# Other matmul durations in the planner of a two-network kernel

## The chip, the core and the metric

The kernel runs on one core of a Trainium2 chip. The metric is the time of one launch on the device in microseconds (us), the median over several runs. Five engines share the work of the core: TensorE (PE) multiplies matrices and transposes, VectorE (DVE) and ScalarE (ACT) work element by element, GpSimd (POOL) does a few element-wise steps, and SyncE (SP) starts the transfers from and to memory. Each engine works its own row of instructions strictly in order; semaphores make it wait for the others.

## The reference

Two networks run one after the other on 256 tokens of width 1024, all in fp32. The first has two layers of three attentions side by side (dilated, latent and differential) and an MLP with squared ReLU. The second has four layers whose mixers are retention, conformer convolution, short convolution and retention again, each followed by such an MLP.

```python
def conformer_conv_mixer(x, w_pw1, b_pw1, w_dw, b_dw, ln_g, ln_b, w_pw2, b_pw2):
    h = x @ w_pw1 + b_pw1
    a, gate = jnp.split(h, 2, axis=-1)
    h = a * jax.nn.sigmoid(gate)
    h = causal_depthwise_conv(h, w_dw) + b_dw
    ...
    hf = (hf - mean) * lax.rsqrt(var + LN_EPS) * ln_g.astype(F32) + ln_b.astype(F32)
    h = jax.nn.silu(hf).astype(x.dtype)
    return h @ w_pw2 + b_pw2

def second_block(x, positions, norm_g, ...):
    for i in range(DEPTH_2):
        ...
        x = x + rms_norm(h, norm_g[i, 1])
        h = squared_relu_mlp(rms_norm(x, norm_g[i, 2]), mlp_w1[i], mlp_w2[i])
        x = x + rms_norm(h, norm_g[i, 3])
    return x
```

## The kernel before

The 256 tokens are two tiles of 128, called t=0 and t=1 here. The weights stream through the core in units of up to 128 x 1024 fp32. A unit arrives in a tile `raw` (4 of them), ACT copies it to `whi` (8), rounded to the faster matmul type fp32r, and DVE subtracts the two to get the rest, `wlo` (8). Lines 716 to 727, `prefetch`, do this. Activations are split in the same way into a high and a low tile `t4k` (lines 801 to 812). A product is then three matmuls: high by high, high by low, low by high. They gather in PSUM tiles `acc` (4) or `wk` (4).

The conformer (lines 1384 to 1513) makes its 1024 channels in 8 blocks of 128. A block's gated input is an `s2k` tile; the 31 taps of its convolution are shared out by the table `CONV` (line 24): ACT multiplies some taps and POOL adds them, PE does some by diagonal matrices (`dg`, `s2k`), and DVE does the others with one `SCALAR_TENSOR_TENSOR s1k<-s2k,cv,s1k` per tap. A last addition `s1k<-s1k,s1k` joins the parts. The blocks are 256 tokens wide except the last ones (third entry 1 in `CONV`), which are done 128 tokens at a time. PE then transposes the channels of one t back (`wk<-ident,s1k`), DVE takes their statistics (`BN_STATS`) and the normalized z (`TENSOR_SCALAR s2k<-wk,col,col`; the second half of z is ACT's), PE transposes z (`wk<-ident,s2k`), ACT applies silu, and the result is split into `t4k`. The product with `w_pw2` (called pw2 here, lines 786 to 799) takes 8 units, first all of t=0 and then all of t=1, and the residual x is updated from it.

No order is written out by hand. Every operation is recorded first, with a cost in ns from `cost` (line 293) that depends on engine, operation and size. `deadlines` (line 366) adds the costs of the recorded PE operations up to a time at which each PE operation is due, and goes back through the dependences to give every other operation a due time `dl`; an operation may not start earlier than 60,000 ns before its due time. `schedule` (line 389) then plays the program through: of each engine's ready operations it takes the one that can start first, and among equals the one that is due first. It hands out the buffers in that order too, and `pe_end` models PE's slower clock after pauses. `emit` (line 536) writes the instructions in that order, so the whole profile carries one line number, 546, and the groups are told apart by their tiles. The numbers behind a tile's name in the orders below are the tile's running number there, and differ between two plans.

Of the kernel before, what the change touches and what calls it, by code (L numbers as in the profile page):

```python
# [18 lines left out]
P = 128  # L19
# [265 lines left out]
class Rec:  # L285
# [7 lines left out]
    def cost(self, op, outs, ins):  # L293
        fn = op.name
        if fn == "dma_start":
            n = max(v.arr.size for v in outs + ins) * 4
            op.dma = n / 360.0
            return 60.0, 2000.0
        o = outs[0]
        n = int(np.prod(o.shape[1:]))  # L300
        n_in = max([int(np.prod(v.shape[1:])) for v in ins] + [n])
        lat = LAT[op.eng]
        psum = any(v.vt.psum for v in ins + outs)
        if op.eng == "tensor":
            if fn == "transpose":
                return 2 * o.shape[1] / 2.4 + 2.5, lat
            f32 = op.kw["lhsT"].vt.dtype == F32
            return ((4 if f32 or n < 256 else 1) * max(n, P)) / 2.4 + 2.5, lat
        if op.eng == "scalar":
            ptr = sum(isinstance(op.kw.get(k), V) for k in ("scale", "bias", "accum_out"))  # L310
            return 94 + n * 0.8333 + 93 * ptr - (43 if psum else 0), lat
        if op.eng == "gpsimd":
            if ALU.pow in (op.kw.get("op"), op.kw.get("op1")):
                return 234 + 230.0 * n, lat
            if fn == "memset":
                return 40 + n * 0.6, lat
            return 160 + n * 2.1, lat
        if fn == "reciprocal":
            return 69 + 6.25 * n, lat
        if fn == "scalar_tensor_tensor":  # L320
            return 129 + 1.042 * n, lat
        if fn == "tensor_scalar":
            ptr = sum(isinstance(a, V) for a in op.args[2:])
            return 69 + 60 * ptr + (1.042 if psum else 0.52) * n, lat
        if fn in ("tensor_copy", "memset"):
            return 69 + (1.042 if psum else 0.52) * n, lat
        return 69 + 1.042 * n_in, lat
# [1334 lines left out]
```

## Time and profile before

| | us |
|---|---|
| median of 3 runs | 1993.25 |
| lowest and highest run | 1992.52, 1994.31 |
| span of the profiled execution | 1991.4 |
| PE busy | 1949.0 (98%) |
| DVE busy | 1335.8 (67%) |
| ACT busy | 1051.1 (53%) |
| POOL busy | 159.1 (8%) |

The span runs from the first to the last instruction of the profiled execution; the runs' times also hold what lies around it, 1.85 us between the span and the median. No time of its own is listed for the profiled execution beside its span. Busy shares are an average over the whole span. Instructions of one engine overlap a little, so a row's duration is somewhat longer than the distance to the next row.

### The profile page before, as it was taken

The numbers are of one execution on the slowest core, as the hardware profiler recorded it, in microseconds if no ns is written. First come the engines' busy times: TensorE is split into PE (matmuls) and PEld (weight loads), VectorE is DVE, ScalarE is ACT, GpSimd is POOL, SyncE is SP. The second block draws the span as 40 slices with busy tenths as digits, with TensorE's granted clock in tenths as the row PEclk, the third lists the DMA queues.
The fourth block names the chain that finished last, engine by engine and source line by source line (L and its number), as shares of the span: only waits on it lengthen the run. The fifth ranks groups of instructions, "written<-read, shape, count | busy, mean of one in ns | idle before, by whom it ended". The sixth has DMA issues, their size and how long they took to land.

```text
span 1991.4 us, 30668 instructions
## 1 busy us (share of the span) xinstructions
PE 1949.0 (98%) x11696; PEld 1721.8 (86%) x11696; DVE 1335.8 (67%) x2169; ACT 1051.1 (53%) x1757; POOL 159.1 (8%) x233
## 2 busy tenths in 40 slices
PE   8999999999999999999997799999999999999998
PEld 7879998878998888899877689989899889888997
DVE  7866556886556776755589975567755577757554
ACT  7555545555545335645486655455545453555452
POOL 2200002100000000000047400000000000000000
PEclk9999999999999999999998899999999999999999
DMA  7256664246555555465631265646465655455552
GB/s 238 85 168 204 188 197 146 76 152 208 189 198 183 174 165 192 165 198 189 210 129 48 80 226 186 200 159 217 164 202 189 201 170 169 160 192 178 191 184 91
DMA packets 95763, 341.44 MB, mean 171 GB/s; under 512 B 10624, under 2 KB 10880, under 8 KB 95616
## 3 DMA queue, kind: packets, MB, share of 16 engines
q1 hardware_dynamic: 95616, 339.49, 52.6%
q8 instruction: 91, 1.49, 0.3%
q14 instruction: 56, 0.46, 0.1%
HBM read 338.40 MB, written 1.05 MB: 170 GB/s over the span
## 4 chain that ended last, share of the span: by engine, by line
PE 90%; DVE 6%; issue 1%; POOL 1%; DMA 1%; ACT 1%; SPq 0%; POOLq 0%; DVEq 0%; ACTq 0%
PE wk L546 47%; PE acc L546 43%; DVE s1k L546 4%; DVE s2k L546 1%; POOL s2k L546 1%; DMA raw<-in_w 1%; ACT s2k L546 0%; DVE wlo L546 0%; DMA x<-in_x 0%; DVE col L546 0%; DVE t4k L546 0%; DVE dg L546 0%; POOL s1k L546 0%; ACT whi L546 0%; SPq L546 0%
## 5 line engine op out<-in xcount | busy, mean ns | idle before, releaser
L546 DVE TENSOR_TENSOR wlo<-raw,whi 128x1024 fp32r<-128x1024 f32 (+3 forms) x639 | 774.0, 1217 | 538.2 <-ACT whi L546 533.6
L546 ACT CAST whi<-raw 128x1024 fp32r<-128x1024 f32 (+3 forms) x639 | 656.5, 1034 | 734.7 <-PE wk L546 374.5
L546 PE MATMUL wk<-t4k,whi 128*128 128x256 f32 x3712 | 662.8, 282 | 12.4 <-DVE s2k L546 8.8
L546 PEld LDWEIGHTS wk<-t4k,whi 128*128 128x128 f32 x3712 | 573.8, 190 | 22.0 <-DVE s2k L546 9.6
L546 PE MATMUL wk<-t4k,wlo 128*128 128x256 f32 x1856 | 510.7, 282 | 0.0
L546 PE MATMUL acc<-whi,r2k 128*128 128x512 f32 x1440 | 410.3, 394 | 0.0
L546 PE MATMUL acc<-whi,t4k 128*128 128x512 f32 (+2 forms) x1312 | 391.4, 387 | 5.9 <-ACT t4k L546 2.1
L546 PEld LDWEIGHTS wk<-t4k,wlo 128*128 128x128 f32 x1856 | 346.6, 190 | 0.1
L546 PEld LDWEIGHTS acc<-whi,r2k 128*128 128x128 f32 x1440 | 264.8, 188 | 54.6
L546 PEld LDWEIGHTS acc<-whi,t4k 128*128 128x128 f32 x1312 | 239.7, 189 | 48.5 <-ACT t4k L546 3.2
L546 PE MATMUL acc<-wlo,r2k 128*128 128x512 f32 x720 | 227.8, 393 | 0.0
L546 PE MATMUL acc<-wlo,t4k 128*128 128x512 f32 (+2 forms) x656 | 227.7, 386 | 0.0
L546 PE MATMUL wk<-whi,t4k 128*128 128x512 f32 x512 | 163.9, 398 | 0.0
L546 PEld LDWEIGHTS acc<-wlo,r2k 128*128 128x128 f32 x720 | 135.2, 188 | 31.1
L546 PEld LDWEIGHTS acc<-wlo,t4k 128*128 128x128 f32 x656 | 123.1, 190 | 20.1
L546 POOL TENSOR_TENSOR col<-col,mhalf 128x1 f32<-128x1 f32 (+1 forms) x48 | 38.3, 806 | 1157.1 <-DVE col L546 1156.8
L546 PEld LDWEIGHTS wk<-whi,t4k 128*128 128x128 f32 x512 | 95.8, 188 | 21.8 <-ACT t4k L546 0.4
L546 PE MATMUL wk<-wlo,t4k 128*128 128x512 f32 x256 | 98.7, 395 | 0.0
L546 PE MATMUL wk<-s2k,s2k 128*128 128x64 f32 (+6 forms) x492 | 85.3, 308 | 4.1 <-DVE s2k L546 3.6
L546 PEld LDWEIGHTS wk<-s2k,s2k 128*128 128x128 f32 (+2 forms) x492 | 72.6, 197 | 16.5 <-DVE s2k L546 4.0
L546 ACT ACTIVATE t4k<-wk,cv 128x128 fp32r<-128x128 f32 x256 | 72.4, 379 | 16.2 <-PE wk L546 15.9
L546 DVE SCALAR_TENSOR_TENSOR t4k<-wk,cv,t4k 128x128 fp32r<-128x128 f32 x256 | 72.4, 343 | 10.5 <-ACT t4k L546 9.6
(126 smaller groups left out, 1366.2 us busy)
## 6 DMA issues: line engine op xcount, KB each, us to landing
raw<-in_w SPq DMA_DIRECT2D x599, 512.0 KB, 4.2
raw<-in_w SPq DMA_DIRECT2D x26, 384.0 KB, 3.2
row<-in_rows SPq DMA_DIRECT2D x11, 512.0 KB, 5.0
raw<-in_w SPq DMA_DIRECT2D x8, 288.0 KB, 2.8
raw<-in_w SPq DMA_DIRECT2D x4, 432.0 KB, 4.8
kcs<-in_kc SPq DMA_DIRECT2D x2, 768.0 KB, 7.4
x<-in_x SPq DMA_DIRECT2D x4, 256.0 KB, 6.3
out_dram<-x SPq DMA_DIRECT2D x4, 256.0 KB, 2.0
```

The costliest lines, as they stand in the source:

```text
L546: op.dma = fn(*[res(a) for a in op.args], **{k: res(a) for k, a in op.kw.items()})
```

## The change

One line of the planner's `cost` becomes another. It gives the duration of a matmul with n output columns, in ns; `f32` is true for full fp32 operands and false for fp32r.

```diff
             if fn == "transpose":
                 return 2 * o.shape[1] / 2.4 + 2.5, lat
             f32 = op.kw["lhsT"].vt.dtype == F32
-            return ((4 if f32 or n < 256 else 1) * max(n, P)) / 2.4 + 2.5, lat
+            return (4 * max(n, 64) / 2.4 + 5.0 if f32 else n * 0.4434 + 4.5), lat
```

| matmul | before, ns | after, ns |
|---|---|---|
| fp32r, 512 columns | 215.8 | 231.5 |
| fp32r, 384 columns | 162.5 | 174.8 |
| fp32r, 288 columns | 122.5 | 132.2 |
| fp32r, 256 columns | 109.2 | 118.0 |
| fp32, 256 columns | 429.2 | 431.7 |
| fp32, 128 columns | 215.8 | 218.3 |
| fp32, 64 columns | 215.8 | 111.7 |

Instructions, operands and arithmetic stay as they are. What changes is the order on the engines and which buffer of a pool an operation gets. Of DVE's rows some 960 operations stand at another place, of PE's some 1990, of ACT's some 520; most moves are by a few places. Three places are shown.

The first is DVE's row in the conformer, around the gated input of the last channel blocks (`s2k<-wk,s1k 128x512`), where the subtractions that make `wlo` of the pw2 units stand. Rows of one tap that repeat are left out. Before, one such subtraction stands there:

```order
L546 TENSOR_TENSOR s1k_821<-s1k_821,s1k_829 128x256
...
L546 TENSOR_TENSOR s1k_553<-s1k_553,s1k_557 128x256
...
L546 TENSOR_TENSOR s1k_214<-s1k_214,s1k_814 128x256
L546 TENSOR_TENSOR s2k_409<-wk_110,s1k_535 128x512
L546 SCALAR_TENSOR_TENSOR s1k_804<-s2k_112,cv,s1k_804 128x256
L546 TENSOR_TENSOR wlo_608<-raw_96,whi_121 128x1024
L546 SCALAR_TENSOR_TENSOR s1k_8647<-s2k_84,cv,wk_165 128x128
```

and after the change four:

```order
L546 TENSOR_TENSOR wlo_156<-raw_96,whi_121 128x1024
L546 SCALAR_TENSOR_TENSOR s1k_833<-s2k_452,cv,s1k_833 128x256
L546 TENSOR_TENSOR wlo_338<-raw_100,whi_425 128x1024
...
L546 TENSOR_TENSOR wlo_418<-raw_86,whi_357 128x1024
L546 TENSOR_TENSOR s2k_421<-wk_133,s1k_541 128x512
...
L546 TENSOR_TENSOR wlo_348<-raw_92,whi_200 128x1024
L546 TENSOR_TENSOR s2k_452<-wk_163,s1k_541 128x512
L546 SCALAR_TENSOR_TENSOR s1k_818<-s2k_108,cv,s1k_818 128x256
L546 SCALAR_TENSOR_TENSOR s1k_541<-s2k_88,cv,wk_133 128x128
```

The three others of the four stood behind t=0's `BN_STATS` before, in the stretch where t=1's last taps run.

The second place is PE's row in the same layer, at the beginning of the pw2 product of t=0. The three `wk<-ident,s1k` are the transposes of t=1's last channel blocks. Before, 19 matmuls of pw2 stand ahead of them, the last ones here:

```order
L546 MATMUL acc_273<-whi_539,t4k_176 128x512
L546 MATMUL acc_129<-whi_539,t4k_176 128x512
L546 MATMUL acc_273<-whi_355,t4k_359 128x512
L546 MATMUL wk_480<-ident,s1k_549 128x128
L546 MATMUL wk_480<-ident,s1k_557 128x128
L546 MATMUL wk_480<-ident,s1k_547 128x128
L546 MATMUL acc_129<-whi_355,t4k_359 128x512
```

and after the change 9:

```order
L546 MATMUL acc_173<-whi_425,t4k_123 128x512
L546 MATMUL acc_173<-wlo_338,t4k_123 128x512
L546 MATMUL acc_275<-whi_425,t4k_123 128x512
L546 MATMUL wk_515<-ident,s1k_560 128x128
L546 MATMUL wk_515<-ident,s1k_8732 128x128
L546 MATMUL wk_515<-ident,s1k_828 128x128
L546 MATMUL acc_275<-wlo_338,t4k_123 128x512
```

The transposes moved from the fourth unit's first product to the second unit's.

The third place is DVE's row at the start, in the first attention layer, where the latent attention's compressed q and kv (`acc`, 384 and 128 columns) are scaled by their norms (`col`). Before:

```order
L546 TENSOR_TENSOR wlo_127<-raw_86,whi_148 128x864
L546 TENSOR_TENSOR wlo_216<-raw_92,whi_121 128x864
L546 TENSOR_SCALAR col_280<-col_137,keep_187 128x1
L546 TENSOR_TENSOR wlo_157<-raw_96,whi_265 128x576
L546 TENSOR_SCALAR col_280<-col_161,keep_192 128x1
L546 TENSOR_SCALAR col_301<-col_286,keep_187 128x1
L546 SCALAR_TENSOR_TENSOR s2k_112<-acc_129,col_137,sm_102 128x384
```

and after the change:

```order
L546 TENSOR_TENSOR wlo_260<-raw_92,whi_121 128x864
L546 TENSOR_TENSOR wlo_156<-raw_96,whi_257 128x576
L546 TENSOR_TENSOR wlo_277<-raw_100,whi_264 128x576
L546 TENSOR_SCALAR col_290<-col_137,keep_191 128x1
L546 TENSOR_SCALAR col_294<-col_281,keep_234 128x1
L546 SCALAR_TENSOR_TENSOR keep_177<-col_113,col_161 128x1
L546 TENSOR_SCALAR col_281<-col_288,keep_191 128x1
L546 TENSOR_SCALAR col_113<-col_296,keep_234 128x1
L546 SCALAR_TENSOR_TENSOR s2k_280<-acc_129,col_137,sm_102 128x384
```

Two 576-wide subtractions now stand ahead of the first `TENSOR_SCALAR`, where one stood behind it. On PE the transposes of `s2k` stand two 288-wide matmuls earlier.

## Rows read from the trace of the kernel before

**Rows 1.** The page: busy us and instructions by engine; then the chain's shares.

```profile
PE 1949.0 (98%) x11696; PEld 1721.8 (86%) x11696; DVE 1335.8 (67%) x2169; ACT 1051.1 (53%) x1757; POOL 159.1 (8%) x233
...
PE 90%; DVE 6%; issue 1%; POOL 1%; DMA 1%; ACT 1%; SPq 0%; POOLq 0%; DVEq 0%; ACTq 0%
```

**Rows 2.** By window: length, busy PE, PEld, DVE, ACT, POOL, clock, DMA, GB/s.

```profile
1050.00:1100.00 50.00, 38.51 (x241) 36.37 (x241) 49.38 (x79) 30.07 (x63) 38.50 (x49) 0.87 0.09 31
1100.00:1150.00 50.00, 39.78 (x191) 31.18 (x191) 45.68 (x93) 32.55 (x76) 17.45 (x33) 0.86 0.32 108
1150.00:1200.00 50.00, 49.94 (x311) 44.13 (x310) 33.98 (x43) 28.40 (x40) 1.46 (x1) 1.00 0.64 211
```

**Rows 3.** Waits of PE by releaser: us in total, times, longest us.

```profile
PE wk L546 <- DVE s2k L546: 14.5, 4, 4.5
PE wk L546 <- DVE s1k L546: 8.4, 5, 3.7
...
PE wk L546 <- POOL s2k L546: 1.0, 5, 0.3
```

**Rows 4.** The chain in order of time: start us, us, what, with its count.

```profile
27.18 5.59 DMA raw<-in_w
...
178.42 5.57 PE acc L546 x24
183.99 5.64 PE wk L546 x48
```

**Rows 5.** DVE's timeline at the start: start us, us, instruction, [idle before, releaser].

```profile
21.04 1.06 DVE L546 TENSOR_TENSOR wlo<-raw,whi 128x864 fp32r<-128x864 f32 x1 [0.42 <-PE acc L546]
22.36 0.21 DVE L546 TENSOR_SCALAR col<-col,keep 128x1 f32<-128x1 f32 x1 [0.26 <-ACT s2k L546]
22.49 0.75 DVE L546 TENSOR_TENSOR wlo<-raw,whi 128x576 fp32r<-128x576 f32 x1
```

**Rows 6.** PE's timeline at the start.

```profile
24.82 0.49 PE L546 MATMUL wk<-ident,s2k 128*128 128x128 f32 x3
```

**Rows 7.** DVE's timeline at the end of the conformer.

```profile
1093.55 0.35 DVE L546 SCALAR_TENSOR_TENSOR s1k<-s2k,cv,wk 128x128 f32<-128x128 f32 x1 [0.62 <-POOL s1k L546]
...
1113.80 0.80 DVE L546 TENSOR_SCALAR s2k<-wk,col,col 128x512 f32<-128x512 f32 x1
1114.52 0.34 DVE L546 SCALAR_TENSOR_TENSOR s1k<-s2k,cv,s1k 128x128 f32<-128x128 f32 x1
...
1119.83 0.68 DVE L546 TENSOR_TENSOR t4k<-s2k,t4k 128x512 fp32r<-128x512 f32 x1
...
1125.09 0.28 DVE L546 TENSOR_TENSOR s1k<-s1k,s1k 128x128 f32<-128x128 f32 x1
```

**Rows 8.** DVE's groups from 1093 to 1136 us: shapes, count, busy us, mean ns.

```profile
L546 DVE TENSOR_TENSOR wlo<-raw,whi 128x1024 fp32r<-128x1024 f32 x7 | 8.7, 1244 | 0.5 <-ACT whi L546 0.5
```

**Rows 9.** PE's timeline at the end of the conformer.

```profile
1118.22 0.80 PE L546 MATMUL acc<-whi,t4k 128*128 128x512 f32 x1 [1.18 <-ACT t4k L546]
1118.82 0.63 PE L546 MATMUL acc<-wlo,t4k 128*128 128x512 f32 x1
1119.24 0.63 PE L546 MATMUL acc<-whi,t4k 128*128 128x512 f32 x1
...
1120.56 1.65 PE L546 MATMUL acc<-whi,t4k 128*128 128x512 f32 x3 [0.26 <-DVE t4k L546]
...
1125.95 0.49 PE L546 MATMUL wk<-ident,s1k 128*128 128x128 f32 x3
...
1134.96 0.50 PE L546 MATMUL acc<-whi,t4k 128*128 128x512 f32 x1 [0.91 <-ACT t4k L546]
...
1137.18 0.72 PE L546 MATMUL acc<-whi,t4k 128*128 128x512 f32 x2 [1.01 <-DVE t4k L546]
```

**Rows 10.** DVE's groups from 1028 to 1062 us.

```profile
L546 DVE SCALAR_TENSOR_TENSOR s1k<-s2k,cv,s1k 128x256 f32<-128x256 f32 x31 | 24.4, 838 | 0.0
L546 DVE TENSOR_TENSOR wlo<-raw,whi 128x1024 fp32r<-128x1024 f32 x3 | 4.7, 1565 | 0.0
```

## The prediction

> **What bounds the kernel now.** I read the busy shares first, then the chain that ended last, then the span in pieces of 50 us, and only then single rows. TensorE (PE) is busy 1949.0 of 1991.4 us and the chain lies on it for 90% [rows 1]. A new order of the same instructions can win or lose only where PE stands still or runs at its lower clock. In most pieces there is no such place: from 1150 to 1200 us PE is busy 49.94 of 50 at a granted clock of 1.00. Two pieces stand out, 1050 to 1100 with 38.51 busy and a clock of 0.87, and 1100 to 1150 with 39.78 and 0.86 [rows 2]. That is the conformer. The reader is to see there that VectorE (DVE) is the full engine instead, 49.38 of 50. The list of PE's waits by releaser says the same: 14.5 us in 4 waits for DVE s2k tiles, 8.4 us in 5 for DVE s1k tiles, and hardly anything else but the load of x at the start; the attention's largest item, POOL s2k, is 1.0 us in 5 waits [rows 3].
>
> **Do the new numbers fit?** In the MLP 24 matmuls of 512 columns take 5.57 us, 232 ns each, and 48 of 256 columns take 5.64, 117.5 ns each [rows 4]. The old formula gives 215.8 and 109.2 ns, the new one 231.5 and 118.0. So the planner's PE becomes some 7% slower and true to the trace. The Trainium skill, page "TensorE: Matmul & The Clock Gate", section "Back-to-back issue gap", speaks against it: it gives about 131 ns for 512 columns in a sustained stream and says that N/2.4 + 2.5, the old formula, over-counts there. By that page the new numbers would be further off, not nearer; this case's trace does not agree, with its 232 ns.
>
> What follows from a truer PE is not that PE gets faster. The planner now thinks that PE has more work ahead of each point, so relative to PE everything on the other engines is due at other moments, and some of it changes place.
>
> **The change part by part.**
>
> MLPs, retention, short convolution: PE has no waits there [rows 2], the instructions are the same, so 0. The last instructions of every engine but POOL stand in the same order, so the tail is 0 as well.
>
> The start (first attention layer). Before, the scaling of the compressed q begins with the `TENSOR_SCALAR col` at 22.36, and one 576-wide wlo of 0.75 us follows it at 22.49, hidden while POOL takes the power [rows 5]. After, two such wlo stand ahead of the first `TENSOR_SCALAR`. They can begin when the 864-wide wlo of 21.04 ends at 22.10 [rows 5] and take 0.7 each, so the `TENSOR_SCALAR` would start at 23.5 instead of 22.36 if both their copies are there by then (+1.2), and at 22.8 if only the first counts (+0.5). PE's three transposes, which met no wait at 24.82 [rows 6], stand two 288-wide matmuls earlier, 2 x 0.13 by width from [rows 4]. Together a wait of 0.6 to 1.3 us. Against it: the chain goes on over a weight load of 5.59 us at 27.18 [rows 4], which begins when a wlo frees its raw tile, and the wlo now run earlier, by up to 0.7. So the start is worth -0.5 to +1.3; I take +0.6. The rest of the attention I put at 0, with 1.0 us either way, the size of its largest waits [rows 3].
>
> The conformer. Here DVE's row is the path. Up to the z of tokens 0-127 (the `TENSOR_SCALAR s2k<-wk,col,col` at 1113.80 [rows 7]) the DVE has three more 1024-wide wlo and three more 128-wide taps ahead of it than before; what was there otherwise is the same set. A wlo here takes 1.244 us [rows 8], so 3 x 1.24 = 3.7, and the three taps, 0.34 each by the row at 1114.52 [rows 7] and overlapping a little, 0.8. Taken off is the idle time of 0.62 at 1093.55, where DVE waited for POOL [rows 7]: a row that comes later meets POOL done. Sum +3.9. PE's first pw2 matmul waits for that z over ScalarE (1.18 us for ACT t4k at 1118.22 [rows 9]), so it moves from 1118.22 to about 1122.1.
>
> In the stretch from 1028 to 1062 three such wlo took 1.565 each, and the 256-wide taps 0.838 [rows 10], while POOL adds products beside them. The moved wlo land further on, between 1081 and 1092, with POOL still at work. I stay with 1.24, since a wlo that takes the slow moment leaves the taps behind it a quicker one; 1.565 is the upper bound, 3 x 0.32 = 1.0 more. The Trainium skill has this in "SBUF — State Buffer", section "Who interferes with whom": a DVE instruction with two SBUF inputs contends with a GpSimd instruction that reads SBUF. The trace agrees, with 1.565 against 1.244.
>
> Then the end of the conformer on PE. The three transposes of tokens 128-255 (`wk<-ident,s1k`, at 1125.95, no wait [rows 9]) stood behind 19 pw2 matmuls and now stand behind 9. PE works its row in order, so all that follows is queued behind them, and they need the last tap's sum. That `s1k<-s1k,s1k` at 1125.09 [rows 7] has one more wlo and one t4k (0.68 at 1119.83, same group) ahead of it: +1.24 +0.6 -0.62 = +1.2, so it ends at 1126.6. PE gets there at 1122.1 + 9 x 0.43 + 0.26 = 1126.3; 0.43 is what a 512-column matmul takes from 1118.82 to 1119.24, PE's level of 1.2 GHz after the waits before it, against 0.23 from [rows 4] at 2.4 GHz. That leaves a wait of 0.3 to 0.5; I take 0.4, and 0 to 2 for the range.
>
> What is given back: before, PE waited 0.91 for ACT t4k and 1.01 for DVE t4k of tokens 128-255 [rows 9]. Their z has the same DVE work ahead of it as before, and their t4k now stands ahead of four 512-wide additions and a column, while PE comes 4.3 us later. Both waits are then over before PE is there: -1.9. Conformer: 3.9 + 0.4 - 1.9 = +2.4, within -3 (below) and +7.
>
> Sum: 0.6 + 2.4 = +3.0 us. On the profiled execution that is 1991.4 + 3.0 = 1994.4 of span; the median of the runs, 1993.25, stands 1.85 over that span, so 1996.25, rounded 1996.2.
>
> **The rivals.** A measurement of this kernel can tell 0.2%, 4.0 us, from no change: under 1989.3 is faster, over 1997.2 slower.
>
> (a) Faster, 1988.8. The three wlo cost nothing, because DVE is held up by POOL in that stretch anyway and the tokens' z comes when it did; then the two waits of 1.92 go, the 0.62 goes, the 1.18 and 0.26 ahead of the first pw2 matmuls go [rows 9], and the start gains its 0.5: -4.5. For it: taps of 0.838 next to a busy POOL show much lost time there. Against it: DVE has hardly a gap from 1050 to 1100 (49.38 of 50), and an instruction that stands in a full row pushes all behind it.
>
> (b) Slower, 2000.5. The early transposes block PE. The three wlo take 1.565 (4.7, +0.8 of taps = 5.5), POOL's idle does not go, and the last sum comes 2.2 later, so PE waits 1.5 at the transposes and runs 8 more matmuls at 0.43 instead of 0.23 (1.6) behind that wait; 1.9 are given back, the start costs 0.6: +7.3. It decides from the point where the last sum ends after PE has done its 9 matmuls; by the sum above the two are 0.3 us apart, so it is near. The lengths of waits after which PE was at its lower level support it (1.18 us, and 0.43 per matmul behind it), the 0.91 and 1.01 with no such stretch behind them speak against it.
>
> (c) No change, 1993.25. The planner's new numbers move rows where other engines have room, and the later z is met by PE having the same total work. For it: 98% of PE. Against it: the three wlo ahead of a z that PE waits for.
>
> **How the numbers follow.** Forecast 0.44, (a) 0.19, (b) 0.20, (c) 0.17. Of the forecast a quarter lies over 1997.2. Slower by over 0.2%: 0.11 + 0.19 = 0.30. Faster: 0.14 of (a). Within 0.2%: 0.33 + 0.17 + 0.05 + 0.01 = 0.56. The range reaches from just under (a) to (b)'s value, 1988.5 to 2000.5, and leaves out half of (b) and the lower part of (a).
>
> **What would show it.** Right: PE busy as before outside the conformer; the row of the first `acc<-whi,t4k` in the conformer some 4 us later against the start of the pw1 matmuls, with three or four wlo rows ahead of the first statistics; no wait for t4k of the second tokens; a wait under 1 us at the three `wk<-ident,s1k`. (a) would show the first pw2 matmul no later than before; (b) a wait of over 1 us at those transposes and matmuls at 0.43 apart behind it. The prediction falls if PE's waits move by more than 2 us in the attention layers, or if DVE's stretch from 1028 to 1093 gets shorter or longer by more than the wlo.

## The result and the profile after

The changed kernel takes 2014.2 us in the median (2012.2 to 2021.84), against 1993.78 before in the same series: a ratio of 1.0112, with a 95% interval of 1.0100 to 1.0124. It is some 20 us slower, where 3 us were forecast. The span of its profiled execution is 2011.1 us against 1991.4.

The page of the changed kernel, to be read beside [rows 1]: PE's busy time first, then the chain by engine and by what it ran on.

```profile
PE 1957.8 (97%) x11696; PEld 1724.6 (86%) x11696; DVE 1326.0 (66%) x2169; ACT 1046.0 (52%) x1757; POOL 155.3 (8%) x233
...
PE 89%; DVE 6%; ACT 2%; POOL 1%; issue 1%; DMA 1%; SPq 0%; DVEq 0%; POOLq 0%; ACTq 0%
PE wk L546 47%; PE acc L546 43%; DVE s1k L546 3%; DVE wlo L546 1%; DVE s2k L546 1%; POOL s2k L546 1%; ACT s2k L546 1%; DVE t4k L546 1%; ACT whi L546 0%; DMA raw<-in_w 0%; POOL col L546 0%; DVE x L546 0%; DMA x<-in_x 0%; ACT s1k L546 0%; ACT t4k L546 0%
```

These shares hide the loss: every share moved by a point at most. Of the 19.7 us of span, 8.8 are in PE's busy time (1957.8 against 1949.0), since slow and short-stalled matmuls count as busy, and 10.9 in its idle time. The waits by releaser say more (compare [rows 3]):

```profile
PE wk L546 <- DVE s2k L546: 23.7, 5, 8.6
PE wk L546 <- DVE s1k L546: 6.3, 6, 3.9
...
PE wk L546 <- POOL s2k L546: 2.2, 5, 0.5
PE wk L546 <- DVE t4k L546: 2.2, 1, 2.2
PE acc L546 <- ACT whi L546: 2.0, 1, 2.0
PE wk L546 <- DVE x L546: 1.8, 4, 0.9
```

The DVE s2k item, the conformer's, went from 14.5 to 23.7, while DVE s1k fell from 8.4 to 6.3. Three items were not there before in this size: t4k with `wk`, x, and POOL s2k, which doubled. All but 0.3 us of these lie outside the conformer.

To see where the time went I summed, stage by stage, what each matmul took beyond the usual distance to the next one for its kind (the 35th percentile over all kernels of this study), from the starts of all 11,696 matmul rows. That counts waits, short stalls and slow stretches alike. A stage ends at the last transposes of x. Each row of these tables comes from the one profiled execution of a kernel, and its sum differs from the difference of the medians by up to 3.7 us ("outside it alone" below: 16.5 against 20.2), so a us or two between two rows says nothing. The loss against before, in us:

| kernel | attention 1 | attention 2 | conformer | short conv. | all other | sum |
|---|---|---|---|---|---|---|
| the changed kernel | 4.6 | 2.5 | 4.8 | 4.1 | 3.4 | 19.4 |

The other 3.4 are mostly 1.6 in the second MLP, 1.1 in the MLP ahead of the conformer and 1.0 in the one behind it. So the loss is not one stall but many, and three quarters of it lie outside the conformer, where the prediction had put 0.6.

**The short convolution** shows a joint in full. PE's timeline, with its wait in brackets:

```profile
1352.68 1.32 PE L546 MATMUL wk<-ident,x 128*128 128x128 f32 x8 [0.85 <-DVE x L546]
1353.83 0.38 PE L546 MATMUL wk<-ident,s1k 128*128 128x128 f32 x2
1356.38 0.77 PE L546 MATMUL wk<-whi,t4k 128*128 128x512 f32 x1 [2.16 <-DVE t4k L546]
1356.94 0.63 PE L546 MATMUL wk<-wlo,t4k 128*128 128x512 f32 x1
1357.37 0.63 PE L546 MATMUL wk<-whi,t4k 128*128 128x512 f32 x1
```

PE waits for x of the second 128 tokens, then for its split, 3.0 us together, and the matmuls behind follow at 0.43 instead of 0.23 us, the 1.2 GHz level: the granted clock is 0.52 from 1356 to 1359.5 us and 0.99 in the 3.5 us behind. Before, the same transposes of x met no wait:

```profile
1335.94 0.60 PE L546 MATMUL wk<-ident,x 128*128 128x128 f32 x4
1336.29 0.48 PE L546 MATMUL wk<-whi,t4k 128*128 128x512 f32 x1
1336.61 0.60 PE L546 MATMUL wk<-ident,x 128*128 128x128 f32 x4
```

Why x comes late is seen on ScalarE. First ScalarE before, then after the change; `s2k<-acc` takes the sums of squares of the MLP's result for the second tokens, from which x is updated:

```profile
1331.30 0.60 ACT L546 ACTIVATE s2k<-acc 128x512 f32<-128x512 f32 x1
...
1332.76 0.60 ACT L546 ACTIVATE s2k<-acc 128x512 f32<-128x512 f32 x1
1333.23 0.21 ACT L546 ACTIVATION_READ_ACCUMULATOR s2k<-acc 128x1 f32 x1
1333.33 2.00 ACT L546 CAST whi<-raw 128x1024 fp32r<-128x1024 f32 x2
```

```profile
1346.60 1.09 ACT L546 CAST whi<-raw 128x1024 fp32r<-128x1024 f32 x1
1347.54 0.65 ACT L546 ACTIVATE s2k<-acc 128x512 f32<-128x512 f32 x1
1348.03 0.25 ACT L546 ACTIVATION_READ_ACCUMULATOR s2k<-acc 128x1 f32 x1
1348.12 0.64 ACT L546 ACTIVATE s2k<-acc 128x512 f32<-128x512 f32 x1
```

After the change a weight copy of 1.09 us stands ahead of the first square; before, both copies stood behind the last. VectorE does the same one step later. Before, and then in the changed kernel:

```profile
1333.56 0.26 DVE L546 TENSOR_SCALAR col<-col,col,keep 128x1 f32<-128x1 f32 x1
...
1334.52 1.40 DVE L546 SCALAR_TENSOR_TENSOR x<-s2k,col,x 128x512 f32<-128x512 f32 x2
```

```profile
1348.84 1.21 DVE L546 TENSOR_TENSOR wlo<-raw,whi 128x1024 fp32r<-128x1024 f32 x1
1349.97 0.26 DVE L546 TENSOR_SCALAR col<-col,col,keep 128x1 f32<-128x1 f32 x1
...
1351.87 1.41 DVE L546 SCALAR_TENSOR_TENSOR x<-s2k,col,x 128x512 f32<-128x512 f32 x2 [0.44 <-POOL col L546]
```

After the change a weight split of 1.21 us stands ahead of the column that the update of x needs. PE is in no hurry for these weights: counted by columns in the rows up to 1346.60, ScalarE had copied 409.4 units and PE had used 403.6, so the copy was for a unit some six ahead. x is needed next.

**The conformer.** PE's timeline at its longest wait, and at the beginning of pw2 (compare [rows 9]), and VectorE's row that explains the first:

```profile
1101.15 1.22 PE L546 MATMUL wk<-s2k,dg 128*128 128x256 f32 x2 [8.59 <-DVE s2k L546]
...
1136.56 0.79 PE L546 MATMUL acc<-whi,t4k 128*128 128x512 f32 x1 [1.19 <-ACT t4k L546]
...
1140.56 0.76 PE L546 MATMUL wk<-ident,s1k 128*128 128x128 f32 x3
```

```profile
1086.38 0.81 DVE L546 SCALAR_TENSOR_TENSOR s2k<-s2k,cv 128x256 f32<-128x256 f32 x1 [4.95 <-ACT s2k L546]
...
1092.17 1.48 DVE L546 TENSOR_TENSOR wlo<-raw,whi 128x1024 fp32r<-128x1024 f32 x1
```

VectorE, which before had no gap above 0.62 us from 1028 to 1093 us [rows 7], runs dry for 4.95 us: it waits for the sigmoid of a gated input, ScalarE's `s2k<-s2k,cv 128x256`. The sigmoid's own input is VectorE's `s2k<-wk,s1k`, done at 1080.70. VectorE's row of it, then ScalarE's rows up to the sigmoid, after the change; and last the sigmoid of the same block before:

```profile
1080.03 0.67 DVE L546 TENSOR_TENSOR s2k<-wk,s1k 128x512 f32<-128x512 f32 x1
```

```profile
1081.14 1.03 ACT L546 CAST whi<-raw 128x1024 fp32r<-128x1024 f32 x1
1082.86 1.33 ACT L546 ACTIVATE s1k<-s2k,cv 128x256 f32<-128x256 f32 x3 [0.69 <-POOL s1k L546]
1084.49 0.51 ACT L546 ACTIVATE s1k<-s2k,cv 128x256 f32<-128x256 f32 x1 [0.30 <-POOL s1k L546]
1084.91 1.03 ACT L546 CAST whi<-raw 128x1024 fp32r<-128x1024 f32 x1
1085.84 0.51 ACT L546 ACTIVATE s2k<-s2k,cv 128x256 f32<-128x256 f32 x1
```

```profile
1071.78 0.51 ACT L546 ACTIVATE s2k<-s2k,cv 128x256 f32<-128x256 f32 x1 [3.33 <-DVE s2k L546]
```

Before, ScalarE stood idle for 3.33 us until the input came and took it at once. After, two weight copies of 1.03 us and four taps, which waited 1.0 us for POOL, stood ahead of the sigmoid, and it began 5.1 us after its input was done. A full engine had become an engine with a hole, and the work behind the hole (the three weight splits, the taps) came later. PE's last transposes of x ahead of the conformer, before and after, give the point to count from:

```profile
1011.92 0.60 PE L546 MATMUL wk<-ident,x 128*128 128x128 f32 x4
```

```profile
1022.72 0.60 PE L546 MATMUL wk<-ident,x 128*128 128x128 f32 x4
```

From there the first pw2 matmul starts after 113.8 us (1136.56) in place of 106.3 (1118.22 in [rows 9]), 7.5 later. Summed over VectorE's rows from the last of these transposes to the z of the first tokens, its idle time grew from 2.5 to 9.2 us, and its work by only 0.9. The three splits and three taps of the forecast do stand ahead of that z, but two of the splits were done before the stretch began, and the 75 taps of 256 columns took 48.0 us in place of 52.1.

### The profile page after: what moved, and what is told of

Read it like the earlier page. It is cut to its first block, busy times and chain, and to the rows that moved or that the text cites. A ratio compares the mean times of both kernels' runs of the same rounds, so it can differ in the third digit from the quotient of the medians.

```text
span 2011.1 us, 30644 instructions
## 1 busy us (share of the span) xinstructions
PE 1957.8 (97%) x11696; PEld 1724.6 (86%) x11696; DVE 1326.0 (66%) x2169; ACT 1046.0 (52%) x1757; POOL 155.3 (8%) x233
## 3 DMA queue, kind: packets, MB, share of 16 engines
HBM read 338.40 MB, written 1.05 MB: 169 GB/s over the span
## 4 chain that ended last, share of the span: by engine, by line
PE 89%; DVE 6%; ACT 2%; POOL 1%; issue 1%; DMA 1%; SPq 0%; DVEq 0%; POOLq 0%; ACTq 0%
PE wk L546 47%; PE acc L546 43%; DVE s1k L546 3%; DVE wlo L546 1%; DVE s2k L546 1%; POOL s2k L546 1%; ACT s2k L546 1%; DVE t4k L546 1%; ACT whi L546 0%; DMA raw<-in_w 0%; POOL col L546 0%; DVE x L546 0%; DMA x<-in_x 0%; ACT s1k L546 0%; ACT t4k L546 0%
## 5 line engine op out<-in xcount | busy, mean ns | idle before, releaser
L546 PEld LDWEIGHTS wk<-t4k,whi 128*128 128x128 f32 x3712 | 575.3, 190 | 19.5 <-DVE s2k L546 10.9
L546 PE MATMUL wk<-whi,t4k 128*128 128x512 f32 x512 | 168.3, 400 | 3.2 <-DVE t4k L546 2.2
L546 POOL TENSOR_TENSOR col<-col,mhalf 128x1 f32<-128x1 f32 (+1 forms) x48 | 33.6, 708 | 1177.0 <-DVE col L546 1171.0
L546 PEld LDWEIGHTS wk<-s2k,s2k 128*128 128x128 f32 (+2 forms) x492 | 72.4, 192 | 16.5 <-DVE col L546 3.6
```

The costliest lines, as they stand in the source:

```text
L546: op.dma = fn(*[res(a) for a in op.args], **{k: res(a) for k, a in op.kw.items()})
```

## The experiments

Every kernel differs from before or from the changed kernel in the planner alone, so all compute the same. Four theories are named in the expectations. M: the old formula's too fast PE gave the plan a margin. C: each new order is a fresh draw, whatever the change. F: the 64-column fp32 price does the harm. Y, formed after the traces of the first two groups: with a true PE the planner lets weight copies and splits go ahead of short chains.

### Which durations, and where they act

The first two kernels change the line for one kind of operand each:

```diff
-return ((4 if f32 or n < 256 else 1) * max(n, P)) / 2.4 + 2.5, lat
+return (((4 if f32 or n < 256 else 1) * max(n, P)) / 2.4 + 2.5 if f32 else n * 0.4434 + 4.5), lat
```

> Only the fp32r matmuls get the fitted duration, the fp32 ones keep the old formula. Theory M (margin): the old formula made PE some 7% too fast in the plan, which left every chain on the other engines a margin on the chip; a plan with a true PE has none. The fp32r matmuls carry nearly all of PE's planned time, so about 2010 to 2016. Theory C (chance): any change of the costs draws a new order, and the time falls anywhere from 1985 to 2020, with no tie to which costs were changed. Theory F (the 64-column fp32 matmul, 215.8 to 111.7 ns, is what harms): about 1994.

Measured: 2016.79 us, 1.0116 (1.0101 to 1.0131), 0.8 us above M's range and far from F's 1994. With fp32 alone (the two branches the other way round):

> Only the fp32 matmuls get the new formula (64 columns 215.8 to 111.7 ns, the others 2.5 ns more); fp32r keeps the old one. Theory M: PE's planned time hardly changes, so 1992 to 1997. Theory F: 2010 to 2016. Theory C: anywhere from 1985 to 2020.

Measured: 2001.81 us, 1.0042 (1.0027 to 1.0057): slower too, but 6.9 of it in the conformer and nothing in the short convolution. F falls. M missed too, by 5 us: it had it at no more than 1997.

In the next the due times are added up with the old durations and only the play-through uses the new ones:

```diff
+op.due = ((4 if f32 or n < 256 else 1) * max(n, P)) / 2.4 + 2.5
+return (4 * max(n, 64) / 2.4 + 5.0 if f32 else n * 0.4434 + 4.5), lat
...
-                t += op.cost
+                t += getattr(op, "due", op.cost)
```

> The due times are added up with the old durations, and only the play-through, which decides when PE is free and what is ready, uses the new ones. If the loss comes from the play-through (theory M), about 2010 to 2016, with PE waiting 2 us for t4k of the second tokens in the short convolution again. If it comes from the priorities that the due times set, about 1994. Theory C: anywhere from 1985 to 2020.

Measured: 2009.15 us, 1.0083 (1.0066 to 1.0100), 0.9 below M's range. PE's waits in it, one line of them:

```profile
PE wk L547 <- DVE t4k L547: 2.2, 1, 2.2
```

The wait of 2.2 us for t4k is there again, so the new play-through is enough to make it, without the new due times. The opposite pairing, new due times with the old play-through, was not run.

### How slow, and how much is chance

```diff
-return ((4 if f32 or n < 256 else 1) * max(n, P)) / 2.4 + 2.5, lat
+return ((4 if f32 or n < 256 else 1) * max(n, P)) / 2.4 + 2.5 + 0.5, lat
```

> The old formula plus 0.5 ns per matmul, 0.3% of PE's planned time: far too little to matter as a margin. Theory M and theory F: 1991 to 1997. Theory C: anywhere from 1985 to 2020, since hundreds of instructions change place here too.

Measured: 1997.36 us, 1.0020 (1.0010 to 1.0029), 0.4 above M's range. Then the whole old formula times a factor:

> The old formula times 1.07 for every matmul and transpose: PE as slow in the plan as the fitted numbers make it (planned PE time 1915.8 us against 1910.2), without the fitted numbers' proportions. Theory M (what counts is how slow PE is in the play-through): 2009 to 2017, with the losses at the same places as in the changed kernel: first attention 3 to 5 us, second 1.5 to 3, short convolution 3 to 5. Theory C (each order is a fresh draw): anywhere from 1990 to 2020, the losses at other places.

Measured: 2011.78 us, 1.0093 (1.0078 to 1.0108). The time and the attentions' losses are as M said; the short convolution lost 2.1, less than its 3 to 5.

> The old formula times 1.03. Theory M: between, 1998 to 2007, if the loss grows with the planned slowness; theory C: no order between 1.00, 1.03 and 1.07.

Measured: 2001.45 us, 1.0041 (1.0026 to 1.0056).

> The old formula times 0.97, PE still faster in the plan. Theory M: outside the conformer no loss, in all 1988 to 1997. Theory C: anywhere from 1990 to 2015.

Measured: 1999.09 us, 1.0033 (1.0021 to 1.0046): 2 us slower than M said, and with losses of 5.0 us outside the conformer, where M had none. Two more nudges, asked later for the spread:

> The old formula minus 0.5 ns per matmul. How much of the 20 us is simply that the order of before is a good draw among its neighbours? If chance is small (a few us, as with plus 0.5 ns: 3.7): 1992 to 1999. If it is as large as the change's own loss: over 2005.

Measured: 1996.0 us, 1.0014 (1.0004 to 1.0023).

> The old formula plus 1 ns per matmul (0.6% of PE's planned time). The same question: 1992 to 2000 if chance is small, over 2005 if it is as large as the loss.

Measured: 1993.93 us, 1.0001 (0.9992 to 1.0010).

So orders that differ from before in nothing that matters take 0.5 to 4 us more, and two that do not make PE slower (x 0.97, fitted fp32 only) take 6 and 8. Chance explains some us, not 20, and the 8 us of x 1.03 alone would prove nothing. From 1.00 over 1.03 to 1.07 and to the fitted numbers the loss grows (0, 8, 19, 20 us), and with 1.07 it sits where the changed kernel has it, although the proportions of the durations are the old ones. Loss against before by stage, in us, worked out as above:

| kernel | attention 1 | attention 2 | conformer | short conv. | all other | sum |
|---|---|---|---|---|---|---|
| changed | 4.6 | 2.5 | 4.8 | 4.1 | 3.4 | 19.4 |
| fitted fp32r only | 5.5 | 2.8 | 3.0 | 4.1 | 7.1 | 22.5 |
| new play-through, old due times | 3.4 | 1.9 | 1.5 | 2.8 | 6.4 | 16.0 |
| old x 1.07 | 4.1 | 2.5 | 2.8 | 2.1 | 4.2 | 15.7 |
| old x 1.03 | 4.3 | 0.6 | -0.5 | 0.5 | 3.3 | 8.2 |
| old x 0.97 | 1.0 | -0.1 | 0.1 | 0.4 | 3.7 | 5.1 |
| fitted fp32 only | 1.7 | 0.0 | 6.9 | 0.0 | 2.0 | 10.6 |
| old + 0.5 ns | 0.2 | -1.2 | 3.7 | 0.4 | 0.0 | 3.1 |
| old - 0.5 ns | 0.0 | 0.7 | 1.9 | 0.2 | 2.2 | 5.0 |
| old + 1 ns | 0.7 | -1.7 | 0.8 | 0.3 | 1.6 | 1.7 |

The reader is to see the sum less the conformer's column. In the first five rows, with a slow planned PE, it is 8.7 to 19.5 us, in the five others, as fast as before or nearly, -0.6 to 5.0. The orders of the tables below keep to this (10.3 to 16.7 and -2.5 to 1.6). Single columns are less clean: at x 1.03 attention 1 loses 4.3, the second attention and the short convolution hardly anything. The conformer's column does not follow the planned slowness: it moves by up to 6.9 us with any change, in both groups. Chance (C) is enough to explain it; outside it the planned slowness (M) tells the orders apart.

### What a true PE takes away: a margin at handoffs, or the order of weight work

Theory M in its plain form says that a handoff to PE needs some tenths of a us more in the plan.

```diff
-TO_PE = 110.0
+TO_PE = 300.0
```

> The fitted durations as in the changed kernel, but the plan's extra delay from any engine to PE (TO_PE) is 300 ns in place of 110. If the loss is a missing margin of some tenths of a us at each handoff to PE, this gives it back: 1995 to 2004. If it is that other work (the weight splits) is already taken up when a short chain becomes ready, a handoff delay changes little: 2008 to 2016.

Measured: 2009.31 us, 1.0084 (1.0068 to 1.0099). The attentions lose less than in the changed kernel (2.4 and -0.8), the short convolution still 3.8, all other stages 9.3. As a whole the remedy fails.

The rows of the short convolution above gave theory Y. The greedy step of `schedule` takes, for an engine, the operation that can start first. With a PE that is too fast in the plan the end of the MLP comes a little sooner, the squares are startable as soon as ScalarE is free, and being due earlier they go first. With a slower PE they are not startable yet at that moment, a weight copy is, and it blocks ScalarE for 1.05 us. This is read from the planner's code and the two orders; no run holds the plan's own times. PE's end need not be all of it: VectorE reads the same two `acc` tiles, the code lets no two engines at one PSUM tile at a time, and these reads (`s2k<-acc,row`) stand ahead of both squares in the changed kernel (1345.97) and behind the first square before (1331.59). On the chip the old order costs nothing: the square began at 1331.30 without a noted wait. The test lets only the weight work step back:

```diff
-                key, s = min((c[1], c[0]) for c in lst if c[0] <= s0 + SLACK.get(e, 0.0))
+                wait = 600.0 if e in ("scalar", "vector") and any(vt.tag == "raw" for vt in ops[min(lst)[1][1]].vts) else 0.0
+                key, s = min((c[1], c[0]) for c in lst if c[0] <= s0 + wait)
```

> The fitted durations, and one more rule in the plan: a weight copy on ScalarE or a weight split on VectorE steps back for up to 600 ns if an operation that is due earlier becomes startable in that time. Theory Y (yield): the old, too fast PE made short chains look startable a little sooner, so that no weight copy or split was put ahead of them; with a true PE the planner fills the gap with one (1.05 us on ScalarE, 1.2 us on VectorE) and the chain behind it comes late. Then this gives back the losses at the joints: short convolution 4 us, second MLPs and conformer head about 3 to 4, part of the attentions, in all 1996 to 2005, and no wait of PE for t4k or x at the joints. If the loss comes from something else that a true PE takes away (theory M without this mechanism), 2009 to 2018.

Measured: 2007.35 us, 1.0072 (1.0055 to 1.0089), 2.4 above Y's range and 1.7 below the other. ScalarE at the same joint, in this kernel:

```profile
1340.88 0.64 ACT L547 ACTIVATE s2k<-acc 128x512 f32<-128x512 f32 x1
...
1342.05 0.60 ACT L547 ACTIVATE s2k<-acc 128x512 f32<-128x512 f32 x1
1342.55 0.19 ACT L547 ACTIVATION_READ_ACCUMULATOR s2k<-acc 128x1 f32 x1
1342.64 1.99 ACT L547 CAST whi<-raw 128x1024 fp32r<-128x1024 f32 x2
```

The copies are behind the squares as before, the short convolution's loss is 0.6 us instead of 4.1, and PE waits there neither for x nor for t4k. The other traces agree. A weight copy stands directly ahead of both squares in the changed kernel and in fp32r only, new play-through, x 1.07, handoff 300 and "outside it alone" below, which lose 2.1 to 4.4 us in the short convolution. In the ten orders with no copy ahead of or between the squares the loss there is at most 0.6; in the two with one copy between them (yield 300, without and with handoff 300) it is 0.8 and 2.0. For the short convolution Y is shown. For the conformer it is not: VectorE's wait for a sigmoid is gone with the rule, but it is absent also in three slow orders without the rule (fp32r only, new play-through, x 1.07). The same rule with half the time:

> The same with 300 ns. Theory Y: part of the way, 1998 to 2009; otherwise 2009 to 2018.

Measured: 2004.68 us, 1.0057 (1.0042 to 1.0072), inside the range, but no less is given back than with 600 ns.

> The old formula with the 300 ns rule. Theory Y: the fast PE of the old formula already keeps the weight work behind the chains, so nothing is left to give back: 1989 to 1999, the spread of a new order in the conformer. If the rule is worth something by itself: under 1988.

Measured: 1991.68 us, 0.9991 (0.9982 to 1.0001), no difference that can be told.

> The old formula with the rule that the weight work steps back for up to 600 ns, where 300 gave 1991.68. If the rule is a gain by itself, 1985 to 1991; if 300 was a neutral redraw, 1990 to 1998.

Measured: 1995.75 us, 1.0012 (1.0003 to 1.0022). On the old formula the rule is a redraw, no gain, as Y says.

The same table for these:

| kernel | attention 1 | attention 2 | conformer | short conv. | all other | sum |
|---|---|---|---|---|---|---|
| fitted, handoff 300 | 2.4 | -0.8 | 3.9 | 3.8 | 9.3 | 18.6 |
| fitted, yield 600 | 3.0 | 1.7 | 1.2 | 0.6 | 5.0 | 11.5 |
| fitted, yield 300 | 5.4 | 2.5 | 1.8 | 0.8 | 3.1 | 13.6 |
| fitted, yield 300, handoff 300 | 4.7 | 1.6 | 2.7 | 2.0 | 2.2 | 13.2 |
| old, yield 300 | 0.3 | -0.2 | -0.8 | 0.1 | -2.7 | -3.3 |
| old, yield 600 | 2.0 | 1.2 | 0.2 | 0.1 | -2.4 | 1.1 |

The last test joins the two remedies:

> The fitted durations with both remedies: the 300 ns rule for the weight work, which gave back the short convolution, and the plan's delay to PE at 300 ns, which gave back half of the attentions (in the run with that alone, 2.4 for 4.6 us and -0.8 for 2.5). If they are two separate causes they add: 1996 to 2003. If they were luck of two orders, it stays at 2004 to 2012.

Measured: 2004.64 us, 1.0059 (1.0044 to 1.0074), no better than the rule alone. The two do not add, and what the handoff delay did for the attentions alone does not come back. In the attentions Y is borne out by the chain and yet not by the time. The chain from 14 to 84 us by what it ran on, before, changed, and with the 600 ns rule:

```profile
by line: PE acc L546 39.9%; PE wk L546 27.5%; DMA raw<-in_w 8.0%; POOL s2k L546 6.4%; DVE s2k L546 5.3%; ACT s2k L546 4.6%; issue 4.4%; POOL col L546 1.4%; DVE col L546 1.2%; DVE wlo L546 1.1%; DVE s1k L546 0.4%; DVEq L546 0.1%; ACTq L546 0
```

```profile
by line: PE acc L546 28.8%; PE wk L546 28.5%; DVE wlo L546 8.3%; POOL s2k L546 8.1%; DMA raw<-in_w 5.6%; ACT whi L546 5.0%; issue 4.1%; DVE t4k L546 3.4%; ACT s2k L546 2.9%; DVE s2k L546 2.5%; POOL s1k L546 1.6%; DVE s1k L546 1.3%; DVE col 
```

```profile
by line: PE acc L547 47.3%; PE wk L547 29.8%; POOL s2k L547 7.1%; DMA raw<-in_w 6.4%; ACT s2k L547 3.7%; DVE s2k L547 2.5%; ACT whi L547 1.5%; issue 1.2%; DVE s1k L547 0.4%; DVE col L547 0.2%; SPq L547 0.0%; POOLq L547 0.0%; ACTq L547 0.0%
```

Weight splits and copies were 1.1% of the chain before, 13.3% after the change, 1.5% with the rule; but attention 1 still loses 3.0 of the 4.6 us. What holds the rest there stays open.

### The conformer and the rest apart

Here the fitted formula holds for the operations recorded by the conformer alone, or for all but those.

```diff
+return (NEW if 8157 <= op.i <= 9313 else OLD), lat
```

(NEW and OLD stand for the two formulas.)

> The fitted durations for the conformer's matmuls alone, the old formula everywhere else. The prediction laid nearly all of the loss there (2.4 of 3.0 us). If that is where it sits, 2008 to 2016. If most of it is at the many handoffs outside (by the stage sums of the changed kernel, 4.8 of 19.4 us are in the conformer): 1995 to 2002.

Measured: 2000.07 us, 1.0033 (1.0020 to 1.0045).

> The opposite: fitted durations everywhere but in the conformer. Outside theory: 2004 to 2012, with the losses in the attentions (4 to 5 and 2 to 3 us) and the short convolution (3 to 4 us) as in the changed kernel. Conformer theory: 1992 to 1998.

Measured: 2013.29 us, 1.0102 (1.0085 to 1.0120), 1.3 above the outside theory's range.

| kernel | attention 1 | attention 2 | conformer | short conv. | all other | sum |
|---|---|---|---|---|---|---|
| in the conformer alone | 1.3 | -0.6 | 4.9 | 0.0 | 0.9 | 6.5 |
| outside it alone | 5.6 | 2.5 | -0.2 | 4.4 | 4.2 | 16.5 |

Each loss is local and comes back by itself: 4.9 and -0.2 for the conformer's 4.8; 5.6, 2.5 and 4.4 for 4.6, 2.5 and 4.1. (By the medians the two losses, 7 and 20 us, add to more than the 20 of the changed kernel.) With the conformer alone, VectorE shows the hole again, 3.35 us in place of 4.95:

```profile
1078.34 0.80 DVE L546 SCALAR_TENSOR_TENSOR s2k<-s2k,cv 128x256 f32<-128x256 f32 x1 [3.35 <-ACT s2k L546]
```

A hole is not the only way to lose here: fitted fp32 only lost 6.9 us in the conformer with no gap of VectorE over 2.0 us, old + 0.5 ns 3.7 with none over 0.6.

## Why the prediction was wrong

The sign was as forecast, the size was not: 20 us instead of 3, outside the range. The right sign owes much to luck, as only 4.8 us of the loss lie in the conformer, where the forecast laid it, and the forecast and its rivals alike had nothing of size outside the conformer.

**The step that failed first** is "PE has no waits there, the instructions are the same, so 0" for MLPs, retention and short convolution. It cost 7.5 us (4.1 in the short convolution, the 3.4 of all other stages). The premise holds, though [rows 2] shows only three pieces: in the trace of before PE has no wait over 0.15 us in any of these stages. The step from there to 0 is what fails. A place without a wait can still be just in time. The squares of the second tokens began on ScalarE at 1331.30 with no idle time noted ahead of them and were followed at once by the chain to x; one copy of 1.09 us in front, one split of 1.21 behind, and PE stood for 3 us and ran slow after. The trace of before had the rows that show it, and the new order had the copy in front; neither was looked at, because the stage's waits were zero.

**The attention at 0, plus or minus 1.0**, and the start at +0.6: measured are 4.6 in the first layer, the start included, and 2.5 in the second. The bound was taken from the largest waits of before, the same fault: what waits now is no bound for what can wait. Nor is a loss always a wait. PE's noted waits over 0.15 us in the two attentions rose only from 2.5 to 4.7 us, while its busy time there rose by 4.3 (126.70 to 128.88 and 125.19 to 127.28), at a granted clock of 1.00 before and after; most of the loss are short stalls that count as busy. So the first premise, that an order can lose only where PE stands still or runs at its lower clock, does not hold either. The start's own mechanism did not show: no wait stands at the three transposes of the compressed q, and PE's first wait of the attention comes later:

```profile
24.04 0.49 PE L546 MATMUL wk<-ident,s2k 128*128 128x128 f32 x3
...
33.13 0.38 PE L546 MATMUL acc<-whi,t4k 128*128 128x288 f32 x1 [1.12 <-ACT s2k L546]
```

**The conformer** at +2.4, measured 4.8, was mis-sized, and by a mechanism that the prediction excluded. Its terms: PE's first pw2 matmul came 7.5 us later against the stage's start, not 3.9, and both waits for t4k of the second tokens went, as forecast. The wait at the three early transposes, put at 0.4, is absent: at 1140.56 they follow the matmul before without a gap, so rival (b) did not come true either. The moved splits took some 1.48 us, between the two bounds of 1.244 and 1.565. But they were not what made the z late: VectorE's work ahead of it grew by 0.9 us, not by 3.7 + 0.8, and its idle time, of which the forecast took off 0.62, grew by 6.7, with a hole of 4.95 us. The text names this as a point at which it falls: "if DVE's stretch from 1028 to 1093 gets shorter or longer by more than the wlo".

**"What follows from a truer PE is not that PE gets faster"** was right, and the new numbers do fit the trace for fp32r, the kind that was looked at; for fp32 of 64 columns they do not (last section). Rival (c) was wrong. What was not drawn from it is the direction. A plan with a truer PE is not neutral for a greedy planner: in the short convolution it put a copy of 1.09 us ahead of a chain that PE was about to need. The forecast treated the new order as a set of single moves to be priced, and priced three of some 3,500.

What stays open: the attentions' 7 us, and how much of the conformer's loss is chance. In nine of the ten orders with a slow planned PE the attentions lose 4.7 to 8.3 us together, in the tenth (handoff 300) 1.6, in the eight others at most 3.2. The 600 ns rule gave back part (4.7 left), the 300 ns rule nothing (7.9), both remedies hardly anything (6.3).

## What to carry to other kernels

In a greedy list scheduler (one that always takes what can start first) a more exact cost need not give a better plan: an underestimate of the bound engine can be what keeps long background work that is due much later (here weight copies of some 1.05 us and splits of 1.2 to 1.5) from starting just ahead of a short chain that the bound engine needs. When costs are refitted, refit the choice with them, for instance by letting background work step back; measure a few plans that differ by a negligible amount first, to know how much a fresh order is worth by chance (0.5 to 4 us here, 8 at most).

When pricing a reorder, a stage with no waits is not a stage with slack. Look for chains whose links follow one another without a gap and see in the new order what stands between the links.

## What the runs showed of the hardware

The new price of the kind that fell most does not fit the trace. In the trace of before the rows of fp32 matmuls with 64 columns follow one another at 111 ns in the median, which looks like the new 111.7. But there are 192 such rows, and the kernel's code (`weigh`) issues 96 such matmuls: an fp32 matmul leaves two rows. One takes some 222 ns (an estimate, 2 x 111), so the old 215.8 was nearly right and the new price is half of what it should be. The other fp32 prices fit by the same count: two rows of 109 ns for 128 columns (218.3), two of some 215 for 256 (431.7).

So the changed kernel's PE is too fast in the plan by 96 x 0.11, an estimated 10.6 us, all in the two attentions. It does not carry the result: the kernel in which both kinds have a price near the measured one is fitted fp32r only, and it is the slowest of all, 2016.79 us. That truer costs gave a slower kernel is the point of the case.
